# An encoder kernel's transposed feed-forward halves: joined behind a later chunk's weight splits, in a buffer of their own

## The chip, the cores and the metric

The kernel runs on one core of a Trainium2 chip. The metric is the device time of one execution in microseconds (us). Before the change three runs took 1138.44, 1139.49 and 1141.58 us, a median of 1139.49. The profiled execution took 1141.82 us, of which the span from its first to its last instruction is 1139.8 us.

## The reference

Two layers of an encoder over 256 tokens of width 1024, in float32. Each layer is a feed-forward block (FFN) at half weight, a mixing block with two kinds of attention, and a second FFN at half weight.

```
def swiglu(x, w_gate, w_up, w_down):
    return (jax.nn.silu(x @ w_gate) * (x @ w_up)) @ w_down
...
    for l in range(DEPTH):
        x = x + 0.5 * swiglu(rms_norm(x, ffn1_norm[l]), ffn1_w_gate[l], ffn1_w_up[l], ffn1_w_down[l])
...
        x = x + merged @ w_out[l]
        x = x + 0.5 * swiglu(rms_norm(x, ffn2_norm[l]), ffn2_w_gate[l], ffn2_w_up[l], ffn2_w_down[l])
```

The hidden width of an FFN is 2816. The change touches the four FFNs alone.

## The kernel before

**Precision and weights.** Every product is made from three matmuls of parts: a float32 value is split into a high part (a copy to the TensorE's rounded float32 format, on ScalarE, line 185) and a low part (the difference, on VectorE, line 186). All weights go through this: SyncE's queue loads 512 KB into one of 4 `raw` buffers (line 143; line 343 where a block row of the down weights is loaded), ScalarE writes `wh`, VectorE writes `wl`, in rings of 6, and TensorE multiplies (lines 171 to 173). A `raw` buffer is loaded again once VectorE is done with it. SyncE's queue is in order: a load or a transpose that waits holds up all that are queued behind it.

**An FFN, first half.** It runs over 11 chunks of 256 hidden columns. For a chunk `c`, `project` multiplies each of the two token tiles `t` by the gate and up weights, 24 matmuls of 512 columns into one of two PSUM banks `g`. Then `glu` takes the bank: ScalarE writes silu of the gate half to `sg` (line 439), VectorE multiplies it by the up half and writes `hh` (line 440). The bank is free for the next `project` but one when `hh` is written. After both tiles `turn(c)` transposes the chunk: ScalarE pulls the 16-bit halves of `hh` apart into `z` (line 318), SyncE's queue issues a crossbar transpose from `z` to `zT` (line 323), and ScalarE joins the halves again into `a` (line 325). Then `hi` and `lo` are split from `a` (lines 185 and 186), for the eight chunks of kinds F and G after four sums and differences on VectorE (line 330). `hh` and `z` take turns in two buffers (tag `xg`).

**An FFN, second half.** `down` multiplies by the down weights. Chunks marked S in the plan `SFGFGGFGGSS` are multiplied plainly; the others (F, G) by a seven-product scheme that needs sums `u` and `v` of the weight blocks (line 347, VectorE) and their splits. For three chunks these are made ahead, during the first half (`prepare`); for the other five on the way, `u` and `v` going through a pool of two buffers (tag `sums`). In the kernel before, `zT` and `a` of the joins take buffers of the same two.

**What sets the order.** TensorE's instructions stand as the code emits them. Those of ScalarE, VectorE, GpSimd and SyncE are put in order at compile time by a scheduler that follows an estimate of the timeline; each engine then runs its list in order and waits where an operand isn't there. `tc.issue_after(x)` makes the scheduler place an instruction behind `x` on its engine.

## Time and profile before

| what | value |
| --- | --- |
| median of the runs (3) | 1139.49 us (1138.44 to 1141.58) |
| the profiled execution | 1141.82 us, span 1139.8 us, 14538 instructions |
| TensorE busy, and its mean granted clock | 1082.4 us (95%), 0.985 |
| VectorE, ScalarE, GpSimd busy | 877.7, 745.8, 113.7 us |
| FFNs, from about | 0 to 208, 385 to 572, 572 to 768, 946 to 1139.8 us |
| mixing blocks, from about | 208 to 385 and 768 to 946 us |

In the profile, PE is TensorE (PEld its weight loads), DVE is VectorE, ACT ScalarE, POOL GpSimd, SPq SyncE's queue. A row of the timeline gives start and duration in us, the engine, the line and operation, output and input, and in brackets the idle time just before it and what ended that. A row of the waits gives a total, a number of times and the longest one. A row of the windows gives a stretch from:to and its length, then for each engine shown its busy us (and its instructions), then the granted clock of TensorE as a share of full speed (PEclk), the share of time that the DMA engines were busy, and GB/s. Durations of matmuls overlap, and their ends are modelled.

### The profile page before, as it was taken

To read this page: it belongs to the slowest core of one execution; us is meant where nothing else is said; L and a number is where in the kernel's file an instruction comes from. 1 tells how busy PE (TensorE), PEld (TensorE's weight loads), DVE (VectorE), ACT (ScalarE), POOL (GpSimd) and SP (SyncE) were. 2 spreads that over 40 slices of the span, in tenths; PEclk is the share of its full clock that TensorE was granted. 3 is DMA by queue.
4 is the path that set the end of the run, shared out by engine and by line. 5 is a ranking of instruction groups with operands and counts; after the bars stand their busy time and mean duration, and the time that the engine had idled before them with its cause. 6 is when DMAs were issued, how large, how long until landed. Compare 5 with 4: busy or idle time off the path is not lost.

```text
span 1139.8 us, 14538 instructions
## 1 busy us (share of the span) xinstructions
PE 1082.4 (95%) x4949; PEld 877.2 (77%) x4949; DVE 877.7 (77%) x1337; ACT 745.8 (65%) x1070; POOL 113.7 (10%) x118
## 2 busy tenths in 40 slices
PE   9989879999999999999998999899999999899988
PEld 7767668888888877777877768688888888677866
DVE  6568769889886748787976876898898866677697
ACT  6567765588773657676556767557887647676752
POOL 1000020044430000000000000002535100000000
PEclk9999989999999999999999999899999999999999
DMA  7868765766654568785666878566666555787753
GB/s 244 208 189 238 221 161 184 206 202 198 190 175 152 174 182 237 229 246 165 207 196 170 236 219 234 166 203 213 191 159 192 184 166 161 210 214 233 237 172 103
DMA packets 145290, 224.15 MB, mean 197 GB/s; under 512 B 54032, under 2 KB 60208, under 8 KB 145216
## 3 DMA queue, kind: packets, MB, share of 16 engines
q1 hardware_dynamic: 145024, 223.14, 66.7%
q8 instruction: 39, 0.64, 0.2%
q14 instruction: 35, 0.29, 0.1%
q0 software_dynamic: 192, 0.08, 0.1%
HBM read 210.59 MB, written 1.06 MB: 186 GB/s over the span
## 4 chain that ended last, share of the span: by engine, by line
PE 33%; DMA 24%; DVE 21%; ACT 12%; issue 9%; SPq 0%; ACTq 0%; POOL 0%; DVEq 0%; POOLq 0%
DMA raw<-in_w_gu 11%; DVE wl L186 11%; DMA zT<-z 8%; PE g L171 6%; PE g L172 6%; PE g L173 6%; ACT wh L185 5%; ACT a L325 3%; DMA raw<-in_w_d 3%; DVE u L347 2%; DVE v L347 2%; ACT z L318 2%; PE acc L172 2%; PE acc L173 2%; PE acc L171 2%
## 5 line engine op out<-in xcount | busy, mean ns | idle before, releaser
L186 DVE TENSOR_TENSOR wl<-raw,wh 128x1024 fp32r<-128x1024 f32 x336 | 405.0, 1219 | 100.4 <-ACT wh L185 99.5
L185 ACT ACTIVATE wh<-raw 128x1024 fp32r<-128x1024 f32 x336 | 344.1, 1041 | 125.3 <-DMA raw<-in_w_gu 82.6
L171 PE MATMUL g<-wh,xh 128*128 128x512 f32 (+1 forms) x976 | 387.0, 396 | 20.0 <-DVE hh L440 18.8
L172 PE MATMUL g<-wl,xh 128*128 128x512 f32 (+1 forms) x976 | 381.7, 391 | 13.9 <-DVE wl L186 13.9
L173 PE MATMUL g<-wh,xl 128*128 128x512 f32 (+1 forms) x976 | 379.7, 389 | 0.0
L171 PEld LDWEIGHTS g<-wh,xh 128*128 128x128 f32 x976 | 184.6, 189 | 65.7 <-DVE hh L440 27.8
L172 PEld LDWEIGHTS g<-wl,xh 128*128 128x128 f32 x976 | 184.9, 189 | 54.7 <-DVE wl L186 22.2
L173 PEld LDWEIGHTS g<-wh,xl 128*128 128x128 f32 x976 | 184.4, 189 | 38.9 <-DVE xl L186 1.0
L325 ACT ACTIVATE a<-zT 128x1024 uint16<-128x1024 uint16 x44 | 60.2, 1369 | 48.9 <-DMA zT<-z 47.9
L171 PE MATMUL acc<-wh,hi 128*128 128x512 f32 x180 | 71.7, 398 | 0.0
L172 PE MATMUL acc<-wl,hi 128*128 128x512 f32 x180 | 71.3, 396 | 0.2
L173 PE MATMUL acc<-wh,lo 128*128 128x512 f32 x180 | 71.1, 395 | 0.0
L177 POOL TENSOR_TENSOR rs_y<-ms,mhalf 128x1 f32<-128x1 f32 x12 | 8.1, 677 | 582.0 <-DVE ms L223 573.3
L318 ACT ACTIVATE z<-hh 128x1024 uint16<-128x1024 uint16 x44 | 46.3, 1052 | 23.6 <-DVE hh L440 23.6
L330 DVE TENSOR_TENSOR a<-a 128x128 f32<-128x128 f32 x128 | 32.6, 286 | 36.1 <-ACT a L325 35.3
L440 DVE SCALAR_TENSOR_TENSOR hh<-g,rs_y,sg 128x256 f32<-128x256 f32 x88 | 42.1, 478 | 20.5 <-ACT sg L439 20.4
L186 DVE TENSOR_TENSOR lo<-a,hi 128x896 fp32r<-128x896 f32 (+1 forms) x44 | 43.0, 977 | 12.1 <-ACT hi L185 11.9
L347 DVE TENSOR_TENSOR u<-raw 128x512 f32<-128x512 f32 x64 | 41.5, 688 | 7.2 <-ACT a L325 7.1
L185 ACT ACTIVATE wh<-v 128x1024 fp32r<-128x1024 f32 x20 | 21.2, 1059 | 38.0 <-DVE v L347 35.4
L185 ACT ACTIVATE corner<-raw 128x512 fp32r<-128x512 f32 x32 | 20.0, 626 | 38.5 <-DMA raw<-in_w_d 35.4
L574 POOL TENSOR_TENSOR S<-S,sm 128x512 f32<-128x512 f32 x32 | 37.2, 1161 | 65.6 <-DVE sm L573 38.2
L439 ACT ACTIVATE sg<-g,rs_y 128x256 f32<-128x256 f32 x88 | 40.0, 455 | 3.2 <-PE g L173 2.9
(186 smaller groups left out, 1534.8 us busy)
## 6 DMA issues: line engine op xcount, KB each, us to landing
raw<-in_w_gu SPq DMA_DIRECT2D x176, 512.0 KB, 4.4
raw<-in_w_d SPq DMA_DIRECT2D x100, 512.0 KB, 4.3
raw<-in_w_in SPq DMA_DIRECT2D x64, 512.0 KB, 4.5
raw<-in_w_out SPq DMA_DIRECT2D x16, 512.0 KB, 3.5
bb<-in_b_gate SPq DMA_DIRECT2D x16, 256.0 KB, 3.5
raw<-in_w_bsw SPq DMA_DIRECT2D x8, 512.0 KB, 3.8
raw<-in_w_bna SPq DMA_DIRECT2D x8, 512.0 KB, 3.6
raw<-in_w_d SPq DMA_DIRECT2D x12, 256.0 KB, 3.6
```

What stands on the lines that cost most here:

```text
L171: nc.tensor.matmul(ps, xh, wh, start=first, stop=False)
L172: nc.tensor.matmul(ps, xh, wl, start=False, stop=False)
L173: nc.tensor.matmul(ps, xl, wh, start=False, stop=last)
L185: linked("act", lambda: nc.scalar.activation(hi, src, AF.Copy))
L186: linked("dve", lambda: nc.vector.tensor_tensor(lo, src, hi.bitcast(F32), ALU.subtract))
L318: nc.scalar.activation(z, hh.bitcast(U16).rearrange("p s (n two) -> p two (s n)", two=2), AF.Copy)
L325: nc.scalar.activation(a[:, :4, :].bitcast(U16).rearrange("p s (n two) -> p two (s n)", two=2), zT.rearrange("p (two s) n -> p two (s n)", ...
L330: nc.vector.tensor_tensor(a[:, to, :], a[:, x, :], a[:, y, :], op)
L347: sub = lambda to, x, y: nc.vector.tensor_tensor(to, x, y, ALU.subtract)
L439: linked("act", lambda: nc.scalar.activation(sg, ps[:, :FC], AF.Silu, scale=rstd[t]))
L440: linked("dve", lambda: nc.vector.scalar_tensor_tensor(h, ps[:, FC:].rearrange("p (i n) -> p i n", i=2), rstd[t], sg.rearrange("p (i n) -> ...
L574: nc.gpsimd.tensor_tensor(S_, S_, sm.unsqueeze(2).to_broadcast([P, T, S]), ALU.mult)
```

## The change

`turn` is cut in two. `send(c)` writes `z` and issues the transpose into `zT`, which now has one buffer of its own. `arrive()` joins the oldest transposed chunk that is still on its way, makes the sums and splits `hi` and `lo`. It is called for chunk `c - 2` right after the weights of chunk `c` have been asked for, and the join is tied behind the last ScalarE split emitted up to there (`last_hi`), which is that of the last weight piece of chunk `c`. The last two chunks are joined in `down`: chunk 9 behind the splits of the first plain chunk's weights, chunk 10 in the seven-product chunk 2. `glu` writes silu straight into `hh`, and VectorE multiplies it there in place; `sg` is gone. Two constants that nothing used are removed. No instruction is added or taken away: ScalarE has 984 and VectorE 1339 listed instructions in both.

```diff
--- before.py
+++ after.py
@@ -42,8 +42,7 @@
 RING = 6
 RAW = 4
 LAG = 3
-H_LAG, NORM_LAG, QK_LAG, P_LAG, V_LAG, M_LAG = 7.9, 4.0, 16, 10, 7.5, 5.5
-LAST_LAG = 6.1
+NORM_LAG, QK_LAG, P_LAG, V_LAG, M_LAG = 4.0, 16, 10, 7.5, 5.5
 MORE = {"Q1": 2, ("sw", 4): 1.5, ("na", 4): 2, ("na", 5): 1.5}
 ORDER = ("Q0 Q1 K0 K1 q1 q0 a5 k0 a5 k1 a3 v0 a1 a5 v1 a3 g0 a1 a5 g1 a4 g2 a0 g3 a0 a4 g4 a1 a5 g5 a4 "
          "g6 a0 g7")
@@ -181,8 +180,10 @@
         step, n = ap.ap[-1]
         return bass.AP(tensor=ap.tensor, offset=ap.offset + step * (n - 1), ap=[*ap.ap[:-1], [-step, n]])
 
+    last_hi = [None]
+
     def split_to(hi, lo, src):
-        linked("act", lambda: nc.scalar.activation(hi, src, AF.Copy))
+        last_hi[0] = linked("act", lambda: nc.scalar.activation(hi, src, AF.Copy))
         linked("dve", lambda: nc.vector.tensor_tensor(lo, src, hi.bitcast(F32), ALU.subtract))
 
     rstd_done = [None]
@@ -289,8 +290,10 @@
         tag, n = ACC[t][d]
         return ps_acc.tile([P, 512], F32, name="acc", tag=tag, bufs=n)
 
-    def out_rows(get, acc, k0, k1, last, w, l, scale, after, rest=None):
+    def out_rows(get, acc, k0, k1, last, w, l, scale, after, rest=None, split=None):
         pieces = [(k, *rows(w, l, k)) for k in range(k0, k1)]
+        if split:
+            split()
         for t in range(T):
             for d in range(2):
                 for k, wh, wl in pieces:
@@ -313,17 +316,24 @@
             hs = {}
             SLOT = ((1, 2), (0, 3))
 
-            def turn(c, hh):
+            on_way = []
+
+            def send(c, hh):
                 z = act.tile([P, 2, 4 * P], U16, name="z16", tag="xg", bufs=2)
                 nc.scalar.activation(z, hh.bitcast(U16).rearrange("p s (n two) -> p two (s n)", two=2), AF.Copy)
+                zT = fp.tile([P, 2 * 4, P], U16, name="zT", tag="zT")
+                nc.sync.dma_start_transpose(zT, z.rearrange("p two n -> p (two n)"))
+                on_way.append((c, zT))
+
+            def arrive():
+                c, zT = on_way.pop(0)
                 m = 4 if PLAN[c] == "S" else 7
                 hi = fp.tile([P, m, P], F32R, name=f"hi{m}", tag=f"hi{m}", bufs=NS if m == 7 else NFC - NS)
                 lo = fp.tile([P, m, P], F32R, name=f"lo{m}", tag=f"lo{m}", bufs=NS if m == 7 else NFC - NS)
-                zT = fp.tile([P, 2 * 4, P], U16, name="zT", tag="sums", bufs=2)
-                nc.sync.dma_start_transpose(zT, z.rearrange("p two n -> p (two n)"))
                 a = fp.tile([P, 8, P], F32, name="a", tag="sums", bufs=2)
-                nc.scalar.activation(a[:, :4, :].bitcast(U16).rearrange("p s (n two) -> p two (s n)", two=2),
-                                     zT.rearrange("p (two s) n -> p two (s n)", two=2), AF.Copy)
+                with tc.issue_after(last_hi[0].ins):
+                    nc.scalar.activation(a[:, :4, :].bitcast(U16).rearrange("p s (n two) -> p two (s n)", two=2),
+                                         zT.rearrange("p (two s) n -> p two (s n)", two=2), AF.Copy)
                 if m == 7:
                     for to, x, y, op in ((4, 0, 3, ALU.add), (6, 1, 0, ALU.subtract), (5, 4, 1, ALU.subtract),
                                          (7, 2, 5, ALU.subtract)):
@@ -370,6 +380,8 @@
                 split_to(*corner, r0[:, 0, :])
                 low = parts(r1)
                 us, vs = stored.get(c) or differences(r0, r1, lambda name, r: parts(r))
+                if on_way and c >= 2:
+                    arrive()
                 half = lambda pair, i: [p[:, i, :] for p in pair]
                 return (("1", 0, corner), ("2", 1, half(low, 0)), ("3", 6, half(low, 1)), ("5", 3, half(us, 1)),
                         ("6", 4, half(vs, 0)), ("4", 2, half(vs, 1)), ("7", 5, half(us, 0)))
@@ -382,7 +394,8 @@
                 while c < NFC:
                     if PLAN[c] == "S":
                         end = NFC if "S" * (NFC - c) == PLAN[c:] else c + 1
-                        out_rows(get, acc, 2 * c, 2 * end, end == NFC, w_d, l, 0.5, after, *rest)
+                        out_rows(get, acc, 2 * c, 2 * end, end == NFC, w_d, l, 0.5, after, *rest,
+                                 split=None if c else arrive)
                         c = end
                         continue
                     final = c == max(PLAN.rindex("F"), PLAN.rindex("G"))
@@ -435,11 +448,9 @@
                 if t == 0:
                     pair[0] = act.tile([P, 4, P], F32, name="hh", tag="xg", bufs=2)
                 h = pair[0][:, 0::3, :] if t else pair[0][:, 1:3, :]
-                sg = fp.tile([P, FC], F32, name="sg", tag="sg", bufs=2)
-                linked("act", lambda: nc.scalar.activation(sg, ps[:, :FC], AF.Silu, scale=rstd[t]))
-                linked("dve", lambda: nc.vector.scalar_tensor_tensor(
-                    h, ps[:, FC:].rearrange("p (i n) -> p i n", i=2), rstd[t], sg.rearrange("p (i n) -> p i n", i=2),
-                    op0=ALU.mult, op1=ALU.mult))
+                gate, up = (ps[:, i * FC:(i + 1) * FC].rearrange("p (i n) -> p i n", i=2) for i in range(2))
+                linked("act", lambda: nc.scalar.activation(h, gate, AF.Silu, scale=rstd[t]))
+                linked("dve", lambda: nc.vector.scalar_tensor_tensor(h, up, rstd[t], h, op0=ALU.mult, op1=ALU.mult))
 
             for c in range(NFC):
                 first = n == 0 and c == 0
@@ -450,6 +461,8 @@
                     pieces = second
                 else:
                     pieces = columns(w_gu, l, c * 512, 512)
+                if c >= 2:
+                    arrive()
                 prep = PREP if n else PREP_FIRST
                 if c in prep:
                     prepare(prep[c])
@@ -458,7 +471,7 @@
                         glu(t, project(t, pieces, 512), pair)
                     elif t:
                         glu(t, both[t], pair)
-                turn(c, pair[0])
+                send(c, pair[0])
 
             down()
```

On ScalarE, in the second FFN of the first layer, from the first chunk's `z` to the second's, the list before:

```order
L318 ACTIVATE z_3805<-hh 128x1024
L325 ACTIVATE a<-zT 128x2x512
L439 ACTIVATE sg<-g,rs_y 128x256
L185 ACTIVATE hi_3807<-a 128x512
L185 ACTIVATE wh<-raw 128x1024 x3
L439 ACTIVATE sg<-g,rs_y 128x256
L185 ACTIVATE wh<-raw 128x1024
L318 ACTIVATE z_3896<-hh 128x1024
```

In these rows `z` is the write of a chunk's halves, `a<-zT` a join, `sg` (`hh` after the change) a silu, `wh` a weight split, `hi` the split of a joined chunk. The list with the change, at the same place:

```order
L323 ACTIVATE z_3781<-hh 128x1024
L452 ACTIVATE hh<-g,rs_y 128x256
L186 ACTIVATE wh<-raw 128x1024 x2
L335 ACTIVATE a<-zT 128x2x512
L186 ACTIVATE wh<-raw 128x1024
L186 ACTIVATE hi_3892<-a 128x512
L452 ACTIVATE hh<-g,rs_y 128x2x128
L186 ACTIVATE wh<-raw 128x1024
L323 ACTIVATE z_3864<-hh 128x1024
```

The join stood right behind its own chunk's `z` and ahead of the next silu; it now stands behind the next chunk's first silu and two weight splits, and the chunk's `z` still stands behind the join of the chunk before.

On VectorE, where the same FFN turns from its first half to its second, the list before, from the last chunk's last weight corner (`corner`) on; `u` and `v` are the sums of weight blocks for chunk 2, and `lo` the low part of the last joined chunk:

```order
L186 TENSOR_TENSOR corner<-raw,corner 128x512
L440 SCALAR_TENSOR_TENSOR hh<-g,rs_y,sg 128x2x128
L186 TENSOR_TENSOR corner<-raw,corner 128x512
L347 TENSOR_TENSOR u<-raw 128x512 x2
L186 TENSOR_TENSOR lo_4804<-a,hi_4803 128x512
L347 TENSOR_TENSOR v<-raw,u 128x512
L186 TENSOR_TENSOR wl<-u,wh 128x1024
L347 TENSOR_TENSOR v<-raw,v 128x512
L347 TENSOR_TENSOR u<-raw 128x512 x2
```

and with the change:

```order
L187 TENSOR_TENSOR corner<-raw,corner 128x512
L357 TENSOR_TENSOR u<-raw 128x512 x2
L187 TENSOR_TENSOR wl<-raw,wh 128x1024 x2
L187 TENSOR_TENSOR lo_4768<-a,hi_4767 128x512
L187 TENSOR_TENSOR wl<-u,wh 128x1024
L187 TENSOR_TENSOR corner<-raw,corner 128x512
L357 TENSOR_TENSOR v<-raw,u 128x512
L453 SCALAR_TENSOR_TENSOR hh<-g,rs_y,hh 128x2x128
L187 TENSOR_TENSOR corner<-raw,corner 128x512
L357 TENSOR_TENSOR v<-raw,v 128x512
L187 TENSOR_TENSOR wl<-v,wh 128x1024
```

The first `u` stood behind the last `hh` and a corner, just ahead of the last joined chunk's `lo`; `u` and `v` now begin ahead of the last `hh`, and the last joined chunk's `lo` comes later than what is shown.

On ScalarE at that place, before:

```order
L439 ACTIVATE sg<-g,rs_y 128x256
L318 ACTIVATE z_4801<-hh 128x1024
L185 ACTIVATE corner<-raw 128x512
L325 ACTIVATE a<-zT 128x2x512
L185 ACTIVATE hi_4803<-a 128x512
L185 ACTIVATE wh<-u 128x1024
L185 ACTIVATE wh<-v 128x1024
```

and with the change:

```order
L186 ACTIVATE wh<-u 128x1024
L186 ACTIVATE corner<-raw 128x512
L452 ACTIVATE hh<-g,rs_y 128x2x128
L186 ACTIVATE corner<-raw 128x512
L323 ACTIVATE z_4751<-hh 128x1024
L186 ACTIVATE wh<-v 128x1024
L186 ACTIVATE wh<-raw 128x1024 x2
L335 ACTIVATE a<-zT 128x2x512
```

The last join stood ahead of the splits of `u` and `v` (`wh<-u`, `wh<-v`); it now stands behind them and behind two weight splits. Outside the FFNs' first halves and these turns, the lists of ScalarE, VectorE, GpSimd and SyncE are as before. On SyncE, the first two transposes of the second FFN stand behind as many weight loads as before (13 and 17), and each later one behind one or two more (the third behind 22, before 20; the last behind 60, before 59).

## The prediction

> **What bounds the kernel now.** I read the page's busy shares first, then the windows stage by stage, then who waited for whom, then the timeline at the stalls.
>
> ```profile
> PE 1082.4 (95%) x4949; PEld 877.2 (77%) x4949; DVE 877.7 (77%) x1337; ACT 745.8 (65%) x1070; POOL 113.7 (10%) x118
> ...
> 208.00:385.00 177.00, 176.34 (x939) 1.00 0.60 180
> 768.00:946.00 178.00, 177.79 (x944) 1.00 0.60 181
> ```
>
> TensorE sets the time. In the mixing blocks (last two rows) it idles 0.9 us in 355 us, at full clock: nothing to win there. So the loss lies in the FFNs. I cut each into three: the first chunks, the middle of the first half, and the turn into `down`, four rows each.
>
> ```profile
> 30.00:72.00 42.00, 38.12 (x158) 0.96 0.77 207
> 402.00:424.00 22.00, 19.75 (x82) 0.92 0.61 158
> 596.00:614.00 18.00, 17.41 (x77) 1.00 0.55 159
> 962.00:980.00 18.00, 17.07 (x76) 1.00 0.52 156
> 72.00:160.00 88.00, 79.58 (x335) 0.98 0.80 213
> 424.00:526.00 102.00, 98.44 (x422) 1.00 0.77 225
> 614.00:720.00 106.00, 98.81 (x423) 1.00 0.79 221
> 980.00:1086.00 106.00, 98.97 (x424) 1.00 0.77 221
> 160.00:174.00 14.00, 8.99 (x22) 0.63 0.43 132
> 526.00:536.00 10.00, 7.17 (x22) 0.83 0.59 182
> 720.00:734.00 14.00, 9.28 (x26) 0.76 0.40 132
> 1086.00:1096.00 10.00, 6.80 (x20) 0.83 0.62 182
> ...
> sum 147.80, PE 142.85; mean PE 28.57
> ```
>
> A window's loss is its length less PE's busy time, plus its length times the missing share of clock (idle and slow time can overlap, so this is a little high). First chunks: idle 3.9 + 2.25 + 0.6 + 0.9, clock 1.7 + 1.8, together 11.1 us. Middle: 8.4 + 3.6 + 7.2 + 7.0, clock 1.8, together 28.0. Turn: 5.0 + 2.8 + 4.7 + 3.2 idle, 5.2 + 1.7 + 3.4 + 1.7 clock, together 27.7. The rest of `down` and the end (last row) lose 5.0. So 66.8 us can be won in the three places at most.
>
> **What the stalls wait for.** First chunks, in the second FFN:
>
> ```profile
> 410.72 1.06 ACT L318 ACTIVATE z<-hh 128x1024 uint16<-128x1024 uint16 x1 [0.76 <-DVE hh L440]
> 417.38 1.34 ACT L325 ACTIVATE a<-zT 128x1024 uint16<-128x1024 uint16 x1 [5.59 <-DMA zT<-z]
> 418.59 0.44 ACT L439 ACTIVATE sg<-g,rs_y 128x256 f32<-128x256 f32 x1
> 419.90 0.80 PE L171 MATMUL g<-wh,xh 128*128 128x512 f32 x1 [2.25 <-DVE hh L440]
> ```
>
> ScalarE stands 5.59 us before the join, the next silu queues behind it, so `hh` is late and TensorE has no bank for 2.25 us. At the turn, in the first FFN:
>
> ```profile
> 160.56 1.35 ACT L325 ACTIVATE a<-zT 128x1024 uint16<-128x1024 uint16 x1 [2.10 <-DMA zT<-z]
> 161.94 1.29 DVE L347 TENSOR_TENSOR u<-raw 128x512 f32<-128x512 f32 x2 [2.76 <-ACT a L325]
> 163.26 1.06 ACT L185 ACTIVATE wh<-u 128x1024 fp32r<-128x1024 f32 x1 [0.70 <-DVE u L347]
> 164.38 0.79 PE L171 MATMUL tp<-wh,hi 128*128 128x512 f32 x1 [3.13 <-ACT wh L185]
> ```
>
> `u` starts the moment the last join ends, because `zT` and `a` hold both buffers of the pool; its split and TensorE follow. In the middle the waits are of two kinds, `hh` late (first four rows, one for each FFN) and `wl` late (last row, over the whole run):
>
> ```profile
> PE g L171 <- DVE hh L440: 4.4, 3, 2.4
> PE g L171 <- DVE hh L440: 0.7, 1, 0.7
> PE g L171 <- DVE hh L440: 3.7, 3, 2.3
> PE g L171 <- DVE hh L440: 3.4, 3, 1.5
> ...
> PE g L172 <- DVE wl L186: 16.7, 20, 1.3
> ```
>
> Of the middle's 26.2 us idle, 12.2 are `hh`; the other 14 are mostly weight parts.
>
> **The change, part by part.** The durations, the landing of the transposes, and a stretch in which TensorE ran full (the windows' columns here are PE, PEld, DVE, ACT, POOL, clock, DMA share, GB/s):
>
> ```profile
> L186 DVE TENSOR_TENSOR wl<-raw,wh 128x1024 fp32r<-128x1024 f32 x336 | 405.0, 1219 | 100.4 <-ACT wh L185 99.5
> L185 ACT ACTIVATE wh<-raw 128x1024 fp32r<-128x1024 f32 x336 | 344.1, 1041 | 125.3 <-DMA raw<-in_w_gu 82.6
> L325 ACT ACTIVATE a<-zT 128x1024 uint16<-128x1024 uint16 x44 | 60.2, 1369 | 48.9 <-DMA zT<-z 47.9
> L330 DVE TENSOR_TENSOR a<-a 128x128 f32<-128x128 f32 x128 | 32.6, 286 | 36.1 <-ACT a L325 35.3
> L440 DVE SCALAR_TENSOR_TENSOR hh<-g,rs_y,sg 128x256 f32<-128x256 f32 x88 | 42.1, 478 | 20.5 <-ACT sg L439 20.4
> L186 DVE TENSOR_TENSOR lo<-a,hi 128x896 fp32r<-128x896 f32 (+1 forms) x44 | 43.0, 977 | 12.1 <-ACT hi L185 11.9
> L347 DVE TENSOR_TENSOR u<-raw 128x512 f32<-128x512 f32 x64 | 41.5, 688 | 7.2 <-ACT a L325 7.1
> L439 ACT ACTIVATE sg<-g,rs_y 128x256 f32<-128x256 f32 x88 | 40.0, 455 | 3.2 <-PE g L173 2.9
> ...
> DMA to landing us min/median/max: 2.7/3.9/6.4
> ...
> 440.00:450.00 10.00, 10.00 (x46) 8.25 (x45) 7.79 (x13) 8.50 (x10) 0.00 (x0) 1.00 1.03 300
> ```
>
> *Join behind weight splits.* A transpose lands 3.9 us after its issue (2.7 to 6.4). Between `z` and its join there now stand one silu and two splits, 0.46 + 2 × 1.04 = 2.5 us; some 1.4 us of the wait stays at the median, up to 3.9. But the silu that frees a bank is no longer behind it. Behind the waiting join are now a split or two, the next silu and the next `z`. That silu's bank is wanted one tile later, 24 matmuls, 5.2 us (46 matmuls take 10 us in the last row above), so a rest of 3.9 us doesn't reach TensorE. I take 10 of the first chunks' 11.1 us.
>
> *Does it drift?* From one `z` to the next ScalarE's chain is: landing 3.9, join 1.4, two or three splits 2.1 to 3.1, silu 0.5, `z` 1.06 (its row above): 9 to 10 us against 10.4 for a chunk's 48 matmuls. It fits, closely.
>
> *`zT` in a buffer of its own.* It is one buffer, so a transpose waits for the join of the chunk before. That join stands ahead of this chunk's `z` on ScalarE, so the wait is over when the transpose may start: nothing. (Were it not, all loads behind it on SyncE's queue would stand too.) In the pool, `u` no longer needs the last join. On VectorE `u` and `v` for chunk 2 begin ahead of the last `hh`; behind that `hh` only half of `v`, a corner and the splits are left, 4 to 5 us on the two engines, while TensorE still has 24 + 21 matmuls of chunks 0 and 1, about 10 us. The turn's wait goes, and with it its clock loss; what is late next is the last join and `u` of chunk 4, with some 19 us of matmuls ahead (chunks 0 to 3). I take 25 of 27.7.
>
> *The middle.* `hh` now stands right behind the earlier chunk's `lo` on VectorE, with `u` after it. I take four fifths of the `hh` waits and the one clock loss, 0.8 × (12.2 + 1.8) = 11 us, and nothing of the weight waits, which the loads set. Bounds: 0, if the loads make `hh` late too, and about 21 (three quarters of 28), if the weight waits were the join's doing.
>
> *Transposes on SyncE's queue.* The later ones stand behind one or two more loads: better for those loads, later for the transpose, and the join has a chunk's time. *Silu into `hh`, product in place.* The same instructions and sizes, 0.46 and 0.48 us. The silu must now wait until `z` has read the buffer, which stands ahead of it on ScalarE anyway: nothing; if that cover went, up to 0.46 us a tile. I add 2 us for small new waits.
>
> Sum: −10 − 25 − 11 + 2 = −44 us. The profiled execution's 1141.82 us (span 1139.8 and 2.0 around it) becomes 1097.8. It lies 2.3 us above the median of the runs, 1139.49, so the median becomes 1095.5.
>
> **The clock, by row and by rule.** The row at 419.90 shows 2.25 us idle, and its window a clock of 0.92: so short a stall was followed by slow matmuls. The mixing blocks, without stalls, kept 1.00. So I let the clock loss go with the stall. The Trainium skill, "TensorE: Matmul & The Clock Gate", section "HAM oscillation — how this bites in real kernels", says that gaps of over about 3.4 us should be avoided, since they bring the clock to half. This trace disagrees: no stall quoted here is over 3.13 us, and 2.25 us had slow matmuls behind it.
>
> **The rivals.**
>
> *The loads bind.* ScalarE waits longer for weights (82.6 us) than for transposes (47.9). If the silu is merely late behind a `wh` in place of the join, the first chunks and the middle stay as they are, and of the turn perhaps 20 come: −20 + 2, 1121.5. Against it: the stretch from 440 to 450 us moved 300 GB/s with TensorE full, more than the 225 of the middle's windows. Chance 0.18.
>
> *The clock stays low.* If the half-clock stretches are not the stalls' doing, idle time goes and slow time stays: of the sum, 0.9 × 11.9 of the turn's, 0.9 × 3.5 of the first chunks' and 0.8 × 1.8 of the middle's, 15 us, don't come: 1110.5. Against it: each short window with such a loss idles over 2 us, and the two that idle under 1 us have 1.00. Chance 0.04. (By the 3.4 us of the Trainium skill's "TensorE: Matmul & The Clock Gate", too, no stall here should cost clock.)
>
> *VectorE becomes the bound: slower.* Six chunks of each first half now carry either `u` or `v`: four `wl` 4.9, two `hh` 1.0, four sums 1.1, `lo` 1.0, two differences 1.4, one low part 1.2: 10.6 us of durations, against 10.4 for the matmuls. Before, a pair was made in longer and shorter chunks. If the late join makes VectorE stand in each of these 24 chunks, every such us is TensorE's. It decides from 2 us a chunk: 24 × 2 = 48 eats the gain. At 2.2 us: 1095.5 + 53 = 1148. For it: VectorE waited 99.5 us for `wh` before. Against: starts are closer than durations, and the same work was done before with VectorE 77% busy. Chance 0.07.
>
> *The stalls only move.* The join is placed as said, but each bank is late for another reason: 1139. The rows at the turn, where one buffer is the cause, speak against it. Chance 0.06. *More goes:* all of the first chunks and the turn and three quarters of the middle, −60: 1079.5, or beyond. Chance 0.07.
>
> **How the numbers follow.** My forecast has 0.58. The range runs from 1079, the middle's upper bound, to 1122, the rival of the loads. Faster or slower count from 0.3%, 3.4 us, about what a measurement of this kernel can tell from no change: faster 0.58 + 0.18 + 0.04 + 0.07 = 0.87, the same 0.06, slower 0.07.
>
> **What would show it.** Right: at the turn no idle of TensorE and a clock near 1.00; `u` no longer ended by `a`; ScalarE's wait for `zT` still there, but no `hh` wait of TensorE behind it; the middle's `wl` waits about as before. Wrong: waits for `raw` that grow by as much as those for `zT` fall (loads), VectorE above 95% in the middle with TensorE waiting for `hh` or `wl` (VectorE), or the turn's idle kept with another releaser.

## The result and the profile after

The changed kernel takes 1086.14 us (median of four runs, 1085.02 to 1088.32) against 1140.53 for the kernel before (four runs, 1138.44 to 1142.23): a ratio of 0.9526, 95% interval 0.9502 to 0.955. It is 54 us faster; 44 were forecast. The profiled execution took 1086.75 us with a span of 1085.0, 54.8 less than the span before.

The page's busy shares, after:

```profile
PE 1059.2 (98%) x4949; PEld 871.0 (80%) x4949; DVE 878.1 (81%) x1337; ACT 747.8 (69%) x1070; POOL 117.2 (11%) x118
```

TensorE has 23.2 us less of busy time for the same 4949 matmuls: of the 54.8 us only 31.9 were gaps (53.1 before, 21.2 after, gaps of over 0.1 us, the 1.6 us ahead of the first matmul among them). Part of the rest is the half clock (mean granted clock 0.985 before, 0.998 after); more on the other part below. The matmuls run in the same order in every kernel here, so each stage can be cut at the same matmuls in each, those at which the prediction's windows of before begin. The windows of after at these cuts: four rows of first chunks, four of the middle, four of the turn, four of the rest of `down` (columns: PE, PEld, DVE, ACT, POOL, clock, DMA share, GB/s).

```profile
30.23:65.90 35.67, 35.67 (x157) 29.21 (x156) 23.71 (x33) 24.83 (x30) 0.00 (x0) 1.00 0.86 238
383.79:401.92 18.13, 18.13 (x81) 15.02 (x80) 12.14 (x17) 12.51 (x15) 0.00 (x0) 1.00 0.75 214
567.21:584.21 17.00, 17.00 (x77) 14.08 (x75) 9.94 (x12) 12.01 (x14) 0.00 (x0) 1.00 0.80 194
920.07:936.84 16.77, 16.77 (x75) 13.89 (x74) 10.84 (x14) 12.23 (x15) 0.00 (x0) 1.00 0.71 203
65.90:146.56 80.66, 76.99 (x335) 62.10 (x334) 67.35 (x97) 61.82 (x72) 0.52 (x1) 1.00 0.84 240
401.92:500.56 98.64, 96.20 (x421) 78.52 (x420) 78.85 (x113) 75.50 (x87) 0.00 (x0) 1.00 0.81 234
584.21:683.91 99.70, 96.79 (x423) 78.91 (x422) 79.56 (x117) 75.02 (x88) 0.00 (x0) 1.00 0.81 233
936.84:1035.59 98.75, 96.58 (x423) 78.99 (x422) 80.09 (x115) 76.10 (x88) 0.00 (x0) 1.00 0.82 237
146.56:151.09 4.53, 4.53 (x22) 3.75 (x20) 4.18 (x5) 2.42 (x3) 1.74 (x3) 1.00 0.74 156
500.56:505.10 4.54, 4.54 (x22) 3.76 (x21) 4.54 (x7) 3.81 (x5) 0.00 (x0) 1.00 0.73 240
683.91:689.58 5.67, 5.67 (x26) 4.70 (x25) 5.61 (x7) 4.71 (x6) 0.00 (x0) 1.00 0.80 246
1035.59:1039.90 4.31, 4.31 (x20) 3.57 (x19) 4.31 (x7) 3.45 (x5) 0.00 (x0) 1.00 0.71 275
151.09:190.00 38.91, 36.37 (x153) 28.92 (x152) 35.95 (x44) 20.57 (x24) 9.51 (x17) 0.96 0.57 189
505.10:541.92 36.82, 34.56 (x149) 27.44 (x147) 34.24 (x41) 19.07 (x21) 0.00 (x0) 1.00 0.58 193
689.58:726.20 36.62, 34.61 (x153) 27.75 (x152) 35.20 (x43) 19.32 (x22) 0.00 (x0) 1.00 0.62 197
1039.90:1079.79 39.89, 39.12 (x172) 31.76 (x170) 35.30 (x44) 16.95 (x19) 0.00 (x0) 1.00 0.42 136
```

The first column after the window is its length, the time for that piece of work. The first chunks and the turns now run with no idle time at full clock: 4.53 us for the 22 matmuls that took 13.94 at the first turn before. The middle still idles. The rest of `down` idles too, 2.5, 2.3, 2.0 and 0.8 us, against 0.1 to 0.7 us before.

Summed over the four FFNs, for this and for the experiments below (us, lengths at the same matmuls; "idle" is the middle's time without a matmul, gaps of over 0.1 us):

```
                      first   middle (idle)   turn   rest of down   turn + rest
before                100.0   401.8 (26.1)    48.0   141.9          189.9
after                  87.6   377.8 (11.1)    19.0   152.2          171.3
e2_own_zt              93.1   406.7 (27.2)    49.4   142.3          191.7
e3_no_tie              97.9   401.6 (25.3)    19.0   153.8          172.9
e5_turn_early          87.6   380.1 (12.2)    45.0   142.2          187.3
e6_one_split           88.1   393.2 (19.0)    19.0   153.1          172.1
e7_behind_next_z       87.3   366.0 ( 2.0)    20.2   151.5          171.7
e8_pool_sums           88.0   377.2 ( 9.8)    19.0   152.6          171.6
e9_early_no_wait       87.3   369.3 ( 3.7)    23.8   143.7          167.6
e10_next_z_prep        87.3   368.5 ( 3.1)    19.0   151.3          170.3
```

From before to after: first chunks −12.4, middle −24.0, turn −29.0 with +10.4 given back in the rest of `down`; all else, the mixing blocks among it, moves by less than 0.3 in sum. The four make −55.0 against −54.8 of the spans.

The waits of after that answer to the prediction's:

```profile
PE g L170 <- DVE hh L453: 10.7, 9, 2.7
PE g L171 <- DVE wl L187: 3.4, 4, 1.6
ACT a L335 <- DMA zT<-z: 24.9, 24, 3.2
ACT wh L186 <- DMA raw<-in_w_gu: 43.0, 46, 2.2
```

ScalarE still waits for `zT`, half as long as before (47.9). Two things were not foreseen: TensorE's wait for `wl` fell from 16.7 to 3.4 us, and ScalarE's for raw gate and up weights from 82.6 to 43.0, though no load was touched. These rows are totals of the run; the account of the middle below reads them by stage. In the middle of the second FFN ScalarE's order now reads like this:

```profile
404.48 1.04 ACT L323 ACTIVATE z<-hh 128x1024 uint16<-128x1024 uint16 x1
405.42 0.94 ACT L186 ACTIVATE hi<-a 128x896 fp32r<-128x896 f32 x1
406.26 0.46 ACT L452 ACTIVATE hh<-g,rs_y 128x256 f32<-128x256 f32 x1
406.62 2.11 ACT L186 ACTIVATE wh<-raw 128x1024 fp32r<-128x1024 f32 x2
409.00 1.38 ACT L335 ACTIVATE a<-zT 128x1024 uint16<-128x1024 uint16 x1 [0.26 <-DMA zT<-z]
```

Between `z` and its join stand an `hi`, the silu and two splits, and of the transpose's time 0.26 us is left to wait.

### The profile page after: what moved, and what is told of

Read it like the earlier page. It is cut to its first block, busy times and chain, and to the rows that moved or that the text cites. A ratio compares the mean times of both kernels' runs of the same rounds, so it can differ in the third digit from the quotient of the medians.

```text
span 1085.0 us, 14545 instructions
## 1 busy us (share of the span) xinstructions
PE 1059.2 (98%) x4949; PEld 871.0 (80%) x4949; DVE 878.1 (81%) x1337; ACT 747.8 (69%) x1070; POOL 117.2 (11%) x118
## 4 chain that ended last, share of the span: by engine, by line
PE 48%; DMA 22%; DVE 14%; ACT 8%; issue 7%; SPq 0%; POOL 0%; ACTq 0%; DVEq 0%; POOLq 0%
PE g L170 11%; PE g L171 11%; PE g L172 11%; DMA raw<-in_w_gu 9%; DMA raw<-in_w_d 8%; DVE wl L187 6%; DMA zT<-z 5%; ACT wh L186 4%; PE acc L171 2%; PE acc L172 2%; PE acc L170 2%; DVE u L357 2%; DVE v L357 2%; ACT z L323 2%; PE po L609 1%
## 5 line engine op out<-in xcount | busy, mean ns | idle before, releaser
L170 PE MATMUL g<-wh,xh 128*128 128x512 f32 (+1 forms) x976 | 383.5, 393 | 11.2 <-DVE hh L453 10.7
L171 PE MATMUL g<-wl,xh 128*128 128x512 f32 (+1 forms) x976 | 377.5, 387 | 0.0
L335 ACT ACTIVATE a<-zT 128x1024 uint16<-128x1024 uint16 x44 | 60.3, 1371 | 25.0 <-DMA zT<-z 24.9
L171 PE MATMUL acc<-wl,hi 128*128 128x512 f32 x180 | 70.7, 393 | 1.6 <-DVE wl L187 1.6
L453 DVE SCALAR_TENSOR_TENSOR hh<-g,rs_y,hh 128x256 f32<-128x256 f32 x88 | 42.1, 478 | 22.3 <-ACT hh L452 22.2
L452 ACT ACTIVATE hh<-g,rs_y 128x256 f32<-128x256 f32 x88 | 40.4, 459 | 17.0 <-PE g L172 16.6
L186 ACT ACTIVATE wh<-v 128x1024 fp32r<-128x1024 f32 x20 | 21.2, 1060 | 35.8 <-DVE v L357 35.7
L171 PEld LDWEIGHTS acc<-wl,hi 128*128 128x128 f32 x180 | 34.0, 189 | 9.7 <-DVE wl L187 2.9
L340 DVE TENSOR_TENSOR a<-a 128x128 f32<-128x128 f32 x128 | 33.0, 283 | 10.3 <-ACT a L335 10.1
```

What stands on the lines that cost most here:

```text
L170: nc.tensor.matmul(ps, xh, wh, start=first, stop=False)
L171: nc.tensor.matmul(ps, xh, wl, start=False, stop=False)
L186: last_hi[0] = linked("act", lambda: nc.scalar.activation(hi, src, AF.Copy))
L335: nc.scalar.activation(a[:, :4, :].bitcast(U16).rearrange("p s (n two) -> p two (s n)", two=2), zT.rearrange("p (two s) n -> p two (s n)", ...
L340: nc.vector.tensor_tensor(a[:, to, :], a[:, x, :], a[:, y, :], op)
L452: linked("act", lambda: nc.scalar.activation(h, gate, AF.Silu, scale=rstd[t]))
```

## The experiments

Three questions: which of the three parts makes the gain, why the middle gained twice what was forecast, and what is left. Each kernel was timed beside runs of the kernel before; ratios are to those. The median of before was 1139.67 us beside the first four, 1141.36 beside the next four and 1140.15 beside the last two.

**e1_inplace: the gate alone.** The kernel before with the new `glu`:

```diff
-                sg = fp.tile([P, FC], F32, name="sg", tag="sg", bufs=2)
-                linked("act", lambda: nc.scalar.activation(sg, ps[:, :FC], AF.Silu, scale=rstd[t]))
+                linked("act", lambda: nc.scalar.activation(h, gate, AF.Silu, scale=rstd[t]))
```

> The kernel before with one part of the change alone: silu written into hh and multiplied in place, no sg. Theory (the in-place gate costs and gains nothing by itself): within 4 us of the kernel before, 1137 to 1144, with the turns into down and the first chunks stalled as before. Rival (sg's two buffers let ScalarE run ahead, and giving them up makes the silu wait for z): 0.2 to 0.5 us a tile, 10 to 40 us slower, with silu rows that wait for VectorE. Second rival (the writes spared make both engines quicker): 5 to 15 us faster.

Measured: 1142.02 us, ratio 1.0024 (1.0003 to 1.0046). That is 0.3 to 5.2 us slower by the interval, so the gate gains nothing by itself. What it does give is room: the two `sg` buffers are 2 KB of a partition, as much as `zT` takes.

**e2_own_zt: the buffer alone.** As e1_inplace, and

```diff
-                zT = fp.tile([P, 2 * 4, P], U16, name="zT", tag="sums", bufs=2)
+                zT = fp.tile([P, 2 * 4, P], U16, name="zT", tag="zT")
```

> As e1_inplace, and zT in a buffer of its own; every join stays where the kernel before has it in the program, without a tie. Theory (the shared pool made the turn's stall, and the join's early place made the others): the turn's 25 us go, about 1115 (1110 to 1120); u at the turn no longer ended by a; ScalarE still waits some 45 us for zT, the first chunks still lose about 11 us and the middle about 28. Rival 1 (all comes from the join's place, the buffer gives nothing): 1136 to 1144, the turn's windows with 3 to 5 us idle as before. Rival 2 (the pool also made the middle's late weights): 1090 to 1105, with the wl waits of TensorE near 4 us instead of 17.

Measured: 1143.05 us, ratio 1.0026 (1.0001 to 1.005). By its time and its turns (49.4 us, 48.0 before) this is Rival 1: the theory, the prediction's own account of the turn, falls. For the first half it is not quite the buffer alone. The joins stand where they stood in the program, but the scheduler put them earlier on ScalarE: 17 of the 44 have two or more splits between `z` and join, against 31 in the kernel before. ScalarE's waits for `zT` rose from 47.9 to 70.7 us and those for gate and up weights fell from 82.6 to 59.6. At the turns the list is that of before. Some rows of VectorE, ScalarE and TensorE at the turn of the second FFN, in time order:

```profile
520.17 0.63 ACT L185 ACTIVATE corner<-raw 128x512 fp32r<-128x512 f32 x1 [1.99 <-DMA raw<-in_w_d]
520.83 0.69 DVE L186 TENSOR_TENSOR corner<-raw,corner 128x512 fp32r<-128x512 f32 x1 [3.75 <-ACT corner L185]
521.44 1.29 DVE L347 TENSOR_TENSOR u<-raw 128x512 f32<-128x512 f32 x2
521.51 1.39 ACT L325 ACTIVATE a<-zT 128x1024 uint16<-128x1024 uint16 x1 [0.71 <-DMA zT<-z]
523.46 1.04 ACT L185 ACTIVATE wh<-u 128x1024 fp32r<-128x1024 f32 x1
524.56 0.49 PE L171 MATMUL tp<-wh,hi 128*128 128x512 f32 x1 [1.33 <-ACT wh L185]
```

`u` no longer waits for the join: it begins at 521.44, before the join does. But on VectorE it stands behind the low part of a corner, which waits 3.75 us for ScalarE's split of that corner, and that split had waited 1.99 us for its load. On ScalarE the split of `u` stands behind the join and its `hi`: `u` is done at 522.73, its split begins at 523.46, and TensorE waits for that split. At the four turns of e2 the split of `u` begins 2.0, 0.7, 0.7 and 0.9 us after `u` is done. The pool was one of several locks on the same door; the join in ScalarE's row is another, and the corner ahead of `u`, with its load, a third.

**e3_no_tie: the place in the program without the tie.** The changed kernel, but

```diff
-                with tc.issue_after(last_hi[0].ins):
-                    nc.scalar.activation(a[:, :4, :]...
+                nc.scalar.activation(a[:, :4, :]...
```

> The changed kernel without the tie: zT of its own, in-place gate, the join written behind a later chunk's loads, but free to be issued when the scheduler likes. Its order puts the joins of the first chunks right behind the silu that follows z, as before the change, and most later ones two splits further. Theory (a join with two splits ahead of it waits little, one without waits 4 to 5 us and makes hh late): between e2_own_zt and the changed kernel: 1095 to 1110, first chunks 8 to 11 us lost again. Rival (place in the program is all, the tie adds nothing): 1084 to 1090. Rival 2 (only the tie matters): as e2_own_zt.

Measured: 1126.57 us, ratio 0.9889 (0.9852 to 0.9926). Slower than the theory's 1095 to 1110, on the way to Rival 2. The turn is as in the changed kernel (19.0 us), since there the last two joins are written behind the first weights of `down`. The first chunks (97.9) and the middle (401.6) are as before the change: of the program's place without the tie hardly anything is left in the first half. ScalarE waits even longer for `zT`, and less for gate and up weights (35.0 us):

```profile
ACT a L334 <- DMA zT<-z: 97.7, 40, 5.2
PE g L170 <- DVE hh L452: 22.0, 26, 2.9
PE g L171 <- DVE wl L187: 14.9, 17, 1.6
```

**e4_prep_as_others.** The changed kernel with

```diff
-PREP_FIRST = {5: 1, 7: 3, 8: 6}
+PREP_FIRST = {3: 1, 5: 3, 7: 6}
```

> The changed kernel with the first FFN preparing its blocks in chunks 3, 5 and 7 like the other FFNs, instead of 5, 7 and 8. What is left of TensorE's stalls in the first FFN after the change is about 2.7 us at 110 us (hh behind the u and v of two preparations close together) and 2.5 us plus half clock at the turn. Theory (the close preparations make both): 4 to 6 us faster than the changed kernel, 1080 to 1083, no gap over 1 us at those places. Rival (the loads of the first chunks are short there, so earlier preparations starve them): slower by 3 to 10 us, 1089 to 1096, with wl or hh waits before 100 us. Rival 2 (the turn's gap is ScalarE waiting for a raw load that would come late either way): 1083 to 1086.

Measured: 1085.68 us, ratio 0.9536 (0.9493 to 0.9578), the same as the changed kernel. In the first FFN the gap at 110 us shrinks from 2.7 to 1.2 us and turn and rest of `down` together from 43.4 to 40.7, but its first chunks take 38.2 us in place of 35.7: the stalls move to earlier chunks, as the rival had it, but at no net cost, so that the time is the one Rival 2 gave. (The second and third FFN, whose code is the same, took 1.5 and 2.3 us more here, which shows how far single executions differ.)

**e5_turn_early: the turn alone undone.** The changed kernel with the last two joins written ahead of `down`:

```diff
-                if on_way and c >= 2:
-                    arrive()
...
-                                 split=None if c else arrive)
+                                 split=None)
...
+            while on_way:
+                arrive()
             down()
```

> The changed kernel with one thing undone: at the turn the last two joins are written ahead of the first weights of down, as in the kernel before; zT keeps its own buffer, the gate its place, the first half its ties. Theory after e2_own_zt (at the turn the split of u stands behind the join on ScalarE, and the join waits for its transpose; a free buffer only lets VectorE form u sooner): the turn's 29 us come back less the 10 us that down then doesn't lose, so 18 to 20 us slower than the changed kernel, 1103 to 1107, with stalls of tp for wh and wl and half clock at the turns. Rival (own buffer and tie were the remedy, as my prediction had it): 1085 to 1089, no such stalls.

Measured: 1104.53 us, ratio 0.9679 (0.9661 to 0.9698): 18.4 us more than the changed kernel. Its four turns (columns: PE, clock, DMA share, GB/s):

```profile
147.72:159.15 11.43, 8.10 (x21) 0.70 0.42 148
505.88:517.32 11.44, 7.92 (x21) 0.70 0.46 156
694.37:707.61 13.24, 9.44 (x27) 0.75 0.46 142
1051.03:1059.95 8.92, 6.53 (x20) 0.81 0.62 199
```

Idle time and low clock are back, with `zT` in its own buffer and the first half as fast as in the changed kernel. So the turn's gain is made by where the last two joins are written: 26.0 us at the turn, of which the rest of `down` gives 10.0 back. The other rows move with them. In e5 `u` stands behind the corner again; at the second turn that corner waits 2.06 us for its load, the join behind it 0.69 for its transpose. In the changed kernel a corner there still waits 1.76 us, but the split of `u` stands ahead of it. How much of the 26.0 us is the join's and how much the corner's was not tried.

**e6_one_split and e7_behind_next_z: how far behind.** In e6 the tie is to the split before the last, so one split stands ahead of the join in place of two. In e7 it is to the `z` of the next chunk:

```diff
-                with tc.issue_after(last_hi[0].ins):
+                with tc.issue_after((last_z if on_way else last_hi)[0].ins):
```

> The changed kernel with each join tied behind the last but one split of the later chunk: one split ahead of it instead of two in the first half. Theory (each us of lead takes a us from ScalarE's wait, and the waits are paid in hh and wl): midway between the changed kernel and e3_no_tie, 1098 to 1112, with zT waits between 25 and 98 us. Rival 1 (a point from which it decides: with any split ahead the silu is in time): 1085 to 1090. Rival 2 (only the full landing time counts): 1118 to 1127, as without the tie.

> The changed kernel with each join tied behind the z of the next chunk, a whole chunk after its own, so that its transpose has long landed; the transpose of the next chunk has to wait for this join, since zT is one buffer. Theory A (ScalarE's last 24.9 us of waiting for zT make the last hh stalls): zT waits under 5 us, TensorE's hh waits from 10.7 to under 5, 1076 to 1083. Theory B (what is left comes from VectorE's order and the loads): 1084 to 1089. Theory C (each transpose now stands 1.4 us longer on SyncE's queue with the loads behind it, and z, join and split come in one block of 3.4 us ahead of the silu): 1090 to 1110, with more waits for raw or for hh.

Measured: e6 1102.50 us, ratio 0.9648 (0.9619 to 0.9677); e7 1079.74 us, ratio 0.9456 (0.9428 to 0.9484). e6 is midway, as the theory had it. e7 bears out theory A: it is the fastest so far, its interval below the changed kernel's. Its profile is of the fastest of its four runs (1075.09 us), so its stages are some us short of a typical run's. The middles of its first two FFNs (columns: PE, clock, DMA share, GB/s; the other two are like the second), and waits of ScalarE and TensorE:

```profile
65.74:142.86 77.12, 76.11 (x335) 1.00 0.87 244
398.33:494.48 96.15, 95.80 (x421) 1.00 0.89 241
```

```profile
ACT z L324 <- DMA zT<-z: 9.1, 5, 2.1
...
PE g L170 <- DVE hh L454: 1.0, 3, 0.5
```

The join never waits. A few `z` do, 9.1 us in all, since one buffer now makes a transpose wait for the join of the chunk before. SyncE's waits ahead of the transposes add up to 66.7 us, less than the 98.9 of the changed kernel: what theory C feared did not come. The four kernels that differ in the tie alone make a series: waits for `zT` of 97.7 (e3), 56.0 (e6), 24.9 (after) and none (e7), and middles of 401.6, 393.2, 377.8 and 366.0 us. Not one for one, but each step down in one is a step down in the other. (Outside the series this does not hold: see e8 and the middle of the kernel before.) The `wl` waits fall too, 14.9, 9.2, 3.4, and 4.9 in e7, where those for `hh` are down to 1.0.

**e8_pool_sums: VectorE relieved.** The changed kernel with the join's four sums on GpSimd:

```diff
-                        nc.vector.tensor_tensor(a[:, to, :], a[:, x, :], a[:, y, :], op)
+                        nc.gpsimd.tensor_tensor(a[:, to, :], a[:, x, :], a[:, y, :], op)
```

> The changed kernel with the four sums of a join on GpSimd instead of VectorE: 33 us less on VectorE, which is 81 to 85% busy in the middle of the first half after the change. Theory (VectorE's fill is what makes the last hh stalls): hh waits from 10.7 to under 5, 1077 to 1083. Rival (its order does, or the loads): 1084 to 1089. Rival 2 (GpSimd is slow on these or slows VectorE beside it): hi and lo later, VectorE's rows longer, 1090 or more.

Measured: 1088.67 us, ratio 0.9546 (0.952 to 0.9572), no faster than the changed kernel. TensorE's `hh` waits are 10.1 us against 10.7. GpSimd took 94.7 us for what had been 33 on VectorE (its busy time went from 117.2 to 211.9), so `hi` came later as well, VectorE's own busy time fell by 17.9 us only, and the run alone would not acquit VectorE. e7 does: there the middle is nearly full, with VectorE at 82% and all sums on it. One more row matters: ScalarE waits 56.0 us for `zT` here, as long as in e6, and the middle takes 377.2 us, as in the changed kernel. Its waits for gate and up weights fell to 14.4 us instead. So a longer wait for transposes cost nothing here, where it took the place of a wait for weights.

**e9_early_no_wait: an early place, the wait taken away.** The series can't say whether the join's wait costs or its place, since both moved. This kernel is e2_own_zt, which gained nothing, with the join tied right behind its own `z`, but reading a tile that is always there (so it leaves out the transposed values):

```diff
-                nc.scalar.activation(a[:, :4, :]...,
-                                     zT.rearrange("p (two s) n -> p two (s n)", two=2), AF.Copy)
+                with tc.issue_after(zi.ins):
+                    nc.scalar.activation(a[:, :4, :]...,
+                                         ident.bitcast(U16)[:, :P].unsqueeze(1).to_broadcast([P, 8, P])...
```

> As e2_own_zt, with each join tied right behind its own z, as early as it can stand, but reading a constant tile (the identity) in place of the transposed halves: the transposes still run, the join waits for none, and the values after it are not those of the reference. Theory (what costs is ScalarE's wait ahead of the join, not the join's place): first chunks, middle and turn lose little, 1074 to 1092. Rival 1 (the place is the cost: join, split and sums standing ahead of the silu and of hh): 1130 to 1145, as e2_own_zt. Rival 2 (the transposes between the loads on SyncE's queue are the cost): 1110 to 1130, with the wl waits as before.

Measured: 1072.30 us, ratio 0.9393 (0.936 to 0.9427), 71 us below e2_own_zt and 2 us below the theory's range. TensorE is busy for 99% of the span. Its waits:

```profile
PE g L171 <- DVE hh L442: 2.9, 3, 1.3
PE g L172 <- DVE wl L186: 2.4, 3, 1.6
```

The transposes still stand between the loads on SyncE's queue, and the joins at the earliest place: in 43 of 44 chunks neither a silu nor a weight split stands between `z` and join, in e2 in 4. First chunks, middle and turn are nearly as fast as in e7, and only the first FFN's turn still stalls. So neither an early place nor the transposes cost by themselves. What is left for the first half is ScalarE's wait, in so far as the rest of its list may be left aside: the scheduler moved other rows too, and a kernel with this list and the real input was not run. At the turns the list differs in what matters there, since `u` and its split now stand ahead of the last corner; for the turn e9 does not single out the wait.

**e10_next_z_prep.** e7 with e4's table.

> e7_behind_next_z with the first FFN's preparations in chunks 3, 5 and 7 as in the other FFNs. Theory (in the first FFN of e7_behind_next_z TensorE idles 1 us at 112 us, 1.4 us behind 144 us and 1.2 us at its turn, all wl late in a stretch where the loads of two close preparations crowd the weights): 1 to 4 us faster than e7_behind_next_z, 1076 to 1079. Rival (as with e4_prep_as_others, stalls move to earlier chunks, where loads are as short): within 2 us of it, 1078 to 1082.

Measured: 1077.01 us, ratio 0.9442 (0.9413 to 0.947). By the medians 2.7 us faster than e7, but the intervals overlap: not told apart. It is the fastest kernel here that computes the reference, about 9 us below the changed kernel.

## Why the prediction was right, and where it was not

**Direction and bound: right.** TensorE set the time, the loss lay in the three places, the mixing blocks did not move, and 1086.14 lies in the range. What was expected to be seen held at the turn (no idle, clock 1.00) and for the first chunks (ScalarE still waits for `zT`, and TensorE does not behind it). One sign did not: the middle's `wl` waits, expected "about as before", went from 13.1 us to none. And that the sum came within 10 us is in part luck: the middle was taken 13.0 us too small, the turn with what follows it 6.4 too large.

**First chunks: −12.4 for −10, right in kind.** e3 shows that the tie does it: without it 97.9 us, with it 87.6. ScalarE's waits for `zT` there are 41.6 us before, 36.8 in e3 and 6.8 after.

**The middle: −24.0 for −11. This is the mis-sized term, and its two parts came the other way round.** The prediction took its 11 us from the `hh` waits. In the four middles these were 12.2 us before and 10.7 after: almost nothing of that came. The failed step is "nothing of the weight waits, which the loads set": TensorE's `wl` waits there, 13.1 us before, went to none. The loads did not fix them. A load lands 4.3 us after its issue at the median before and 4.4 after, and the same loads left 11.1 us of idle time in the middle with the tie and 25.3 without it (e3).

Nor was it the join's wait that was taken away here. Of the 47.9 us that ScalarE waited for `zT` before, only 3.4 lie in the middles: the list shown ahead of the prediction is of a first chunk, and in the later ones nearly all joins already stood behind two or more splits. What ScalarE waited for in the middles was gate and up weights, 74.1 us. After the change it is 17.3 us for `zT` and 35.8 for weights. In the middle of the second FFN, before:

```profile
ACT wh L185 <- DMA raw<-in_w_gu: 18.2, 13, 3.2
ACT a L325 <- DMA zT<-z: 1.4, 3, 0.7
```

and after:

```profile
ACT wh L186 <- DMA raw<-in_w_gu: 10.7, 12, 1.9
ACT a L335 <- DMA zT<-z: 4.7, 5, 2.5
```

The length of the middle goes roughly with the sum of the two waits over the four FFNs, not with either: 77.5 us before, 86.6 in e2, 87.2 in e3, 74.0 in e6, 56.1 in e8, 53.1 after, 42.7 in e9, 32.1 in e7. So e3 shows that the middle's gain needs the tie; why weights reach ScalarE sooner than in the kernel before is open. One candidate is that a late split also holds its raw buffer, so that the next load starts late. That fits the traffic in the middle of the second FFN, 225 GB/s before and 234 after, but no run tried the buffers apart, nor the tie with `zT` still in the pool. The upper bound, 21 "if the weight waits were the join's doing", was short as well: the 28.0 us taken as the middle's whole loss were too few. The same matmuls took 401.8 us before, 366.0 in e7 and 368.5 in e10, so 33 us or more were to be had.

**Why the loss was read too low.** Length less busy time leaves out what each stall costs beside its gap. The middle of the second FFN before, by TensorE's timeline:

```profile
481.35 0.39 PE L172 MATMUL g<-wl,xh 128*128 128x512 f32 x1
481.57 0.39 PE L173 MATMUL g<-wh,xl 128*128 128x512 f32 x1
482.22 0.50 PE L171 MATMUL g<-wh,xh 128*128 128x512 f32 x1 [0.26 <-ACT wh L185]
483.48 0.50 PE L172 MATMUL g<-wl,xh 128*128 128x512 f32 x1 [0.76 <-DVE wl L186]
```

Matmuls start 0.22 us apart and are shown 0.39 long, since they overlap. At 482.22 the gap is shown as 0.26, but the starts are 0.65 apart, 0.43 more than in a full row; and the first after a gap lasts 0.50. These two stalls cost 0.2 and 0.3 us beside their gaps, counted as busy. Over the four middles TensorE's busy time is 375.6 us before and 363.9 in e7 for the same matmuls; of these 11.7 us the half clock, by the prediction's own figure, is 1.8.

**The turn: −18.6 net for −25, and by another mechanism.** "In the pool, `u` no longer needs the last join" is true and, as e2 shows, worth nothing by itself. What counts is where the last two joins are written (e5: 26.0 us at the turn); with that, `u` and its split moved ahead of the last join, of the last `hh` and of a corner that waits for its load. Whether the later place would do without the buffer was not tried: with `zT` in the pool of two, the transposes and the sums would wait for each other.

"What is late next" had been given 19 us of cover; it was late all the same: the rest of `down` loses 10.4 us more than before. That is not simply the price of a turn without a stall. In e9 the last three turns are full, and the rests behind them take 34.3, 35.8 and 38.5 us, against 36.8, 36.6 and 39.9 in the changed kernel and 34.7, 34.1 and 39.0 before. The kernels of the table that join ahead of `down` (before, e2, e5, e9) have rests of 141.9 to 143.7 us, those that join in it 151.3 to 153.8. So the two joins' work in `down` is the likelier cause; no run tried it alone.

**The small terms.** The in-place gate at nothing: near enough (e1, 0.3 to 5.2 us slower). `zT`'s one buffer at nothing: right. The +2 us for new small waits is not seen apart from `down`'s. "It fits, closely" on drift: right, and e7 shows that a whole chunk of lead fits too.

**The rivals.** The loads bind: no; e7 and e9 ran the same loads with 2.0 and 3.7 us of idle time in the middle. (That the waits for `raw` fell says little: in e3 they fell to 35.0 us, and the middle gained nothing.) VectorE the bound: no; it was busy 78.85 of 98.64 us in the middle of the second FFN, and e7 filled TensorE with VectorE at 82%. The clock stays low: no, 0.998 over the whole run. More goes: the measured −54 lies between the forecast's −44 and this rival's −60, and it is the middle that went further (−24.0 for the rival's −21).

## What to carry to other kernels

A wait on an engine that runs its list in order is paid by all that is queued behind it, not only by the next row. Read such waits stage by stage: the 47.9 us for transposes lay almost all in the first chunks and at the turns, and in the middle the same engine waited for weights. And read all of an engine's waits for transfers together, since one can take the other's place (e3, e8). The cheapest remedy is distance, and it can be measured: move the waiting instruction back until its wait is gone (97.7, 56.0, 24.9, 0 us here), and replace its input by one that is always ready to see whether its place costs (1143 to 1072 us, with the list around it changed too). Before calling stalls "the loads' doing", ask whether the loads themselves land later. And a stage's possible gain is better read from the time of the same matmuls where they run full than from busy time, which hides part of every stall.

## What the runs showed of the hardware

The half clock does not follow a stall's length. The clock records lie on a grid of 3.41 us, and what counts is TensorE's idle time inside one grid window. Before, three windows of the grid in the second FFN (columns: PE, clock, DMA share, GB/s):

```profile
416.19:419.60 3.41, 1.45 (x7) 1.00 0.57 183
419.60:423.01 3.41, 3.11 (x7) 0.50 0.19 25
423.01:426.43 3.42, 3.42 (x16) 1.00 0.84 264
```

And after, around the longest stall that it has left, 2.72 us at 110.15:

```profile
108.11:111.52 3.41, 2.04 (x10) 1.00 0.91 244
111.52:114.94 3.42, 2.07 (x9) 1.00 0.61 182
114.94:118.35 3.41, 3.41 (x17) 1.00 0.81 238
```

The first idles 1.96 us of its window, and the next window runs at half clock. The second, longer stall falls across two windows with 1.37 and 1.35 us idle, and nothing follows. Over the profiles of before, after and the ten experiments there are 3778 such windows at full clock, with the idle time of each added up from TensorE's rows: all 26 that idle over 1.75 us had half clock behind them, none of those under 1.60 us, and two of the nine between. So it tips at about half a window. The Trainium skill, "TensorE: Matmul & The Clock Gate", section "What's actually happening", tells of a free-running window of 3413 ns; the grid agrees. Clusters of stalls under 1 us reach the half as well as one long stall does: at the second turn before, gaps of 0.86, 0.96 and 0.76 us, close together, have the half-clock window from 532.24 on behind them. That fits where most of the clock loss lay, at the turns, and that e3, with as much idle time as the kernel before (47.9 and 53.1 us of gaps), ran at 0.997 against 0.985.
